# A streaming-encoder block on one Trainium2 core: the layer-norm boundaries between its stages are issued in another order, and the last whole feed-forward group stays in PSUM

## The chip, the core and the metric

The program runs on one core of a Trainium2 chip. TensorE (PE) multiplies 128 x 128 blocks into PSUM, VectorE (DVE) and ScalarE (ACT) do elementwise work, GpSimd (POOL) elementwise work in SBUF, and SyncE (SP) and ACT issue DMA transfers. Each engine works through its own queue in order. The metric is the device time of the whole program in microseconds (us), the median of several runs; smaller is better.

## The reference

One layer over 256 tokens of width 2048, in float32, with three sublayers, each closed by a layer norm:

```
x <- LN1(alpha*x + 1/2 * g1 * SwiGLU_1(mod1(x)))      feed-forward, D_FF = 5632
x <- LN2(alpha*x +       g2 * W_out[ mLSTM(u) || RG-LRU(u) ])   u = mod2(x)
x <- LN3(alpha*x + 1/2 * g3 * SwiGLU_2(mod3(x)))      feed-forward, D_FF = 5632
mod_s(x) = LayerNorm_noaffine(x) * (1 + scale_s(c)) + shift_s(c)
shift, scale, gate = silu(c) @ w_ada + b_ada
```

So between two sublayers the result y of the last product is scaled by the gate and added to x, x is normalized with gain and bias, normalized again without them, transposed, and scaled and shifted into `u`, which is the input of the next sublayer's first product.

## The kernel before, in words

The 256 tokens are two blocks (t = 0, 1) of 128 partitions. Every float32 weight tile (128 x 2048, 1 MB) is loaded by SP into one of four `raw` buffers (`load`, L80) and split into two float32r tiles: `hi` is a cast on ACT (L94), `lo` the rest, a subtraction on DVE (L96). A product is three matmuls (hi x hi, lo x hi, hi x lo). Activations are kept split and transposed in `uh` and `ul`. There are three pairs of `hi`/`lo` buffers; `spare` (two of six `slot` tiles) and the halves of `uh`/`ul` serve as more where a tile must be held. When a tile is in `fine` mode it is split in four pieces of 512 columns.

`w_ada`, from which shift, scale and gate come, is 144 further tiles of 1 MB (`ada_tile`, L163: one reducing DVE step each). `tick` puts them between the weight loads at a rate per stage (`RAMP_RATE`, `FFN1_RATE`, `MIX_RATE`, `FFN2_RATE`).

A feed-forward stage (`ffn`) takes its 44 column tiles in groups of eight; the last group has four. `g1` makes the hidden tiles of a group (`pg`, `pv`), `g2` multiplies them by the second weight into PSUM banks `py`, which DVE adds to `yacc` in SBUF (L599). When the last whole group has been added, `residual` multiplies `yacc` by the gate and adds it to x (L287, L288, both on POOL there). The last four tiles' share, the products `tl`, goes to `boundary`.

`boundary` runs three times: FFN1 to mixer, mixer to FFN2, and at the end of the kernel, where nothing follows. `products(t)` are the last products of block t. `take(t, n)` takes a 512-wide quarter of them: times the gate, added to x, and its statistics. `norm(t)` normalizes x with gain `ln_g` and bias `ln_b`: three quarters on DVE, the fourth on ACT and POOL, and `bn_stats` again for the second norm; `start_n`/`finish_n` make the normalized block `n`; `u_of(t, n, k)` transposes a quarter (512 columns, four transposes, `tu`) and scales it into `uh`/`ul`; `mov_t` multiplies the group by a tile of the next stage's weights (12 matmuls, PSUM bank `o` in the mixer, `fg` in FFN2). For block 0 these are done group by group, with the takes of block 1 between them; then comes the norm of block 1 and its groups. One or two of the four weight tiles that are not split ahead (`late`) are split between the groups.

The order of most instructions on an engine is found by a scheduler; those issued through `V`, `A`, `G` and `T` (`Pinned`, L108) keep the order in which they are written.

## Time and profile before

| | |
|---|---|
| median of 3 runs | 2080.53 us (2080.49 to 2081.13) |
| the profiled execution | 2079.97 us, its span 2078.2 us |
| PE busy | 1949.3 us, 94% of the span |
| DVE, ACT, POOL busy | 1434.1, 837.4, 132.7 us |
| PE's mean granted clock | 0.97 |
| moved by DMA | 513.27 MB, 247 GB/s |

The profile is of one execution. Busy times are sums of single instructions' spans; a wait is an engine's idle time, put down to what released it. Where all steps go through a helper, they have its line: L118 is every pinned instruction, so a row is told by the names of what it writes and reads (`x<-x,rsp,ln_b` is the bias step of the norm). Windows are stretches of the span. The granted clock is the share of its full rate that PE was given. The span in 40 slices of 52 us shows PE nearly full but for slices 0 and 1, 15 and 16, 24 and 25, and the last: the start, the two boundaries with a stage behind them, and the end.

### The profile page before, as it was taken

Reading aid. Unit: us, or ns where it says so; the run is one execution under the profiler, and the core shown is the slowest. Engines: PE = TensorE matmul, PEld = TensorE weight load, DVE = VectorE, ACT = ScalarE, POOL = GpSimd, SP = SyncE. Lnnn points to the kernel's source line nnn. Section 1 sums busy time; section 2 is a strip of 40 time slices with the busy share of each in tenths; the row PEclk is TensorE's granted clock in tenths of the full one; section 3 lists DMA queues with packets and bytes.
Section 4 is the critical chain, followed back from the end, with each engine's and each line's share of the span. In section 5 each row is a group of like instructions: output and inputs, shape, how many; then the busy total and the mean of one; then the engine's idle time right before and its main releaser. Section 6 shows DMA issues by size and latency. Waiting matters only on the chain. (4 is left out here: it accounts for less than half of the span.)

```text
span 2078.2 us, 30197 instructions
## 1 busy us (share of the span) xinstructions
PE 1949.3 (94%) x13068; PEld 1800.0 (87%) x13068; DVE 1434.1 (69%) x1287; ACT 837.4 (40%) x788; POOL 132.7 (6%) x111
## 2 busy tenths in 40 slices
PE   7999999999999995599999996799999999999996
PEld 6899998899998974399999884699999899899984
DVE  7998898988878797468876875355444544544558
ACT  5433344443333333443843343433343333333341
POOL 0000000000000071200000112000000000000024
PEclk9999999999999997799999998899999999999998
DMA  9998889998998983266687572366555555555552
GB/s 369 353 352 299 311 310 355 363 355 338 358 348 337 352 299 126 94 248 239 223 301 271 192 270 81 120 228 238 203 185 184 194 188 183 185 183 180 184 196 87
DMA packets 72709, 513.27 MB, mean 247 GB/s; under 512 B 8448, under 2 KB 8576, under 8 KB 10880
## 3 DMA queue, kind: packets, MB, share of 16 engines
q1 hardware_dynamic: 69984, 501.25, 65.5%
q10 hardware_dynamic: 2592, 10.09, 1.3%
q8 instruction: 102, 1.67, 0.3%
q14 instruction: 31, 0.25, 0.0%
HBM read 509.22 MB, written 2.10 MB: 246 GB/s over the span
## 5 line engine op out<-in xcount | busy, mean ns | idle before, releaser
L163 DVE CUSTOM_DVE_ANT_0 ada<-ada,scb,badac 128x2048 f32<-128x2048 f32 x144 | 341.8, 2376 | 20.4 <-DMA ada<-in_w_ada 18.3
L258 PE MATMUL pg<-uh,lg 128*128 128x256 f32 x960 | 272.0, 283 | 0.6 <-DVE lg L96 0.5
L96 DVE TENSOR_TENSOR lw<-rw,hw 128x2048 fp32r<-128x2048 f32 x80 | 185.7, 2321 | 125.4 <-ACT hw L94 125.3
L258 PE MATMUL pv<-uh,lv 128*128 128x256 f32 x960 | 271.8, 283 | 0.0
L256 PE MATMUL pg<-uh,hg 128*128 128x256 f32 x960 | 271.7, 283 | 0.0
L257 PE MATMUL pv<-ul,hv 128*128 128x256 f32 x960 | 271.7, 283 | 0.0
L256 PE MATMUL pv<-uh,hv 128*128 128x256 f32 x960 | 271.7, 283 | 0.0
L257 PE MATMUL pg<-ul,hg 128*128 128x256 f32 x960 | 271.7, 283 | 0.0
L268 PE MATMUL py<-lw,hth 128*128 128x512 f32 x640 | 250.2, 391 | 4.7 <-DVE lw L96 4.5
L269 PE MATMUL py<-hw,htl 128*128 128x512 f32 x640 | 249.2, 389 | 0.0
L267 PE MATMUL py<-hw,hth 128*128 128x512 f32 x640 | 242.7, 390 | 0.0
L96 DVE TENSOR_TENSOR lv<-rv,hv 128x2048 fp32r<-128x2048 f32 x68 | 155.8, 2291 | 123.4 <-ACT hv L94 123.3
L94 ACT CAST hw<-rw 128x2048 fp32r<-128x2048 f32 x80 | 152.7, 1911 | 215.5 <-DMA rw<-in_w 71.0
L96 DVE TENSOR_TENSOR lg<-rg,hg 128x2048 fp32r<-128x2048 f32 x60 | 137.5, 2292 | 106.4 <-ACT hg L94 106.4
L94 ACT CAST hv<-rv 128x2048 fp32r<-128x2048 f32 x68 | 129.4, 1905 | 194.7 <-PE pg L257 76.1
L258 PEld LDWEIGHTS pg<-uh,lg 128*128 128x128 f32 x960 | 184.2, 192 | 1.2 <-DVE lg L96 1.2
L256 PEld LDWEIGHTS pg<-uh,hg 128*128 128x128 f32 x960 | 184.2, 192 | 0.3
L257 PEld LDWEIGHTS pg<-ul,hg 128*128 128x128 f32 x960 | 184.2, 192 | 0.3
L258 PEld LDWEIGHTS pv<-uh,lv 128*128 128x128 f32 x960 | 184.3, 192 | 0.0
L256 PEld LDWEIGHTS pv<-uh,hv 128*128 128x128 f32 x960 | 184.3, 192 | 0.0
L257 PEld LDWEIGHTS pv<-ul,hv 128*128 128x128 f32 x960 | 184.3, 192 | 0.0
L94 ACT CAST hg<-rg 128x2048 fp32r<-128x2048 f32 x60 | 114.2, 1904 | 172.2 <-PE pv L257 108.3
(387 smaller groups left out, 4313.7 us busy)
## 6 DMA issues: line engine op xcount, KB each, us to landing
ada<-in_w_ada SPq DMA_DIRECT2D x144, 1024.0 KB, 5.8
rw<-in_w SPq DMA_DIRECT2D x80, 1024.0 KB, 4.8
rg<-in_w SPq DMA_DIRECT2D x60, 1024.0 KB, 5.0
rv<-in_w SPq DMA_DIRECT2D x60, 1024.0 KB, 4.8
rra<-in_w_r SPq DMA_DIRECT2D x48, 1024.0 KB, 5.5
rs<-in_w_s SPq DMA_DIRECT2D x32, 1024.0 KB, 4.9
rwo<-in_w_out SPq DMA_DIRECT2D x16, 1024.0 KB, 4.8
ro<-in_w_vo SPq DMA_DIRECT2D x8, 1024.0 KB, 4.9
```

Source lines behind the costliest of these rows:

```text
L94: act.copy(cut(hi, w), like(raw[:, w], hi))
L96: low.tensor_sub(cut(lo, w), like(raw[:, w], lo), cut(hi, w).bitcast(F32))
L163: nc.vector.tensor_tensor_reduce(raw, raw, scb, 1.0, badac[:, s, j, kt:kt + 1], ALU.mult, ALU.add, adac[:, s, j, kt:kt + 1])
L256: nc.tensor.matmul(ps, hi[:, w], uh[:, k0 + j, :], start=st, stop=False)
L257: nc.tensor.matmul(ps, hi[:, w], ul[:, k0 + j, :], start=False, stop=False)
L258: nc.tensor.matmul(ps, lo[:, w], uh[:, k0 + j, :], start=False, stop=sp)
L267: nc.tensor.matmul(o, acth[:, k0 + j, tk], cut(hi, w), start=first and j == 0, stop=False)
L268: nc.tensor.matmul(o, acth[:, k0 + j, tk], cut(lo, w), start=False, stop=False)
L269: nc.tensor.matmul(o, actl[:, k0 + j, tk], cut(hi, w), start=False, stop=last and j == 3)
```

## The change

1. *Last whole group in PSUM.* `g2_kept` replaces `g2` for group 4: its products go into eight banks `tl`, one for each block and quarter, which stay open, and the last four tiles' products are added there. The group's `yacc` adds are gone; `yacc` times gate goes into x one group earlier, now on DVE, without `w_ada` tiles beside it.
2. *The norm.* All four quarters are DVE steps. The bias step also writes the sum of its result (`accum_out`), and ACT sums the squares of (x + `sb`), `sb` being minus the mean of the bias; from both come mean and variance of the second norm. `bn_stats` for it are gone.
3. *The order.* `norm` and `takes` are generators, and `front` sets how many of block 1's steps stand between block 0's groups: its takes and its norm. Two quarters are transposed before group 0's products, and the products of a group stand behind the `u` steps of the next. The late weight tiles come in quarters, `hi` on ACT and `lo` on POOL.
4. *Loads.* `ln_g` and `ln_b` are loaded through SP, behind the weight tiles that are split ahead.
5. *Elsewhere.* The scaling of x is pinned on ACT and moved behind the first projections of the mixer; the `og` steps of the mixer come behind the boundary's last pinned instructions (`behind`). `w_ada` rates: FFN1 0.9 to 0.85, mixer 0.45 to 0.55; the shifts and scales of the next sublayer are completed before the boundary.

How the instructions move, first on PE behind the first boundary's last `tl` product. `tu` are the transposes of a quarter, `o` the products of the mixer's first tile, `ho`/`lo` its split weights. Before:

```order
L267 MATMUL tl_7221<-uh,hth_6258 128x512
L268 MATMUL tl_7221<-ul,hth_6258 128x512
L269 MATMUL tl_7221<-uh,htl_6259 128x512
L118 MATMUL tu_0_7275<-ident,n_7257 128x128 x4
L267 MATMUL o_7274<-ho_7136,uh 128x512
L268 MATMUL o_7274<-lo_7137,uh 128x512
```

And with the change:

```order
L279 MATMUL tl_6727<-uh,htl_6274 128x512
L120 MATMUL tu_0_7217<-ident,n_7213 128x128 x4
L120 MATMUL tu_1_7222<-ident,n_7213 128x128 x4
L120 MATMUL tu_2_7239<-ident,n_7213 128x128 x4
L277 MATMUL o_7214<-ho_7074,uh 128x512
L278 MATMUL o_7214<-lo_7075,uh 128x512
```

Three quarters are transposed ahead of the first product; the fourth follows two matmuls into the second group. Next DVE at the same boundary, from the end of block 0's first norm to the first quarter of `n` (`gy` and `sts` of 120 belong to block 1's takes). Before:

```order
L118 SCALAR_TENSOR_TENSOR x<-x,rsp_7238,ln_b_7074 128x512
L118 BN_STATS stp_7243<-x 128x6 x2
L118 BN_AGGR mvn_7258<-stp_7243 128x2
L118 TENSOR_TENSOR gy_7267<-tl_7182,gate 128x512
L118 TENSOR_TENSOR x<-x,gy_7267 128x512
L118 TENSOR_SCALAR n_7257<-x,mvn_7258,rsn_7262 128x512
L118 TENSOR_SCALAR u_0_7280<-tu_0_7275,adac 128x128
```

And with the change, where the four bias steps in a row and a take of block 1 stand ahead of this:

```order
L120 TENSOR_REDUCE tot_7197<-sq_7176 128x2
L120 TENSOR_SCALAR tot_7197<-tot_7197 128x2
L120 TENSOR_TENSOR tot_7197<-tot_7197,sb_7025 128x1
L120 SCALAR_TENSOR_TENSOR tot_7197<-tot_7197 128x1
L120 TENSOR_TENSOR gy_7209<-tl_6725,gate 128x512
L120 TENSOR_TENSOR x<-x,gy_7209 128x512
L120 BN_STATS sts_120<-x 128x6
L120 TENSOR_SCALAR n_7213<-x,tot_7197,rsn_7204 128x512
```

The statistics behind the bias steps are gone, and with the take ahead of these rows two of block 1's stand before `n`, one on each side of the four small steps on `tot`. Last ACT, in block 0's groups at that boundary. Before:

```order
L118 ACTIVATE n_7257<-x,nbn_7264,rsn_7262 128x512 x3
L118 ACTIVATE u_0_7280<-tu_0_7275,adac 128x128 x3
L294 ACTIVATE x<-x 128x2048
L118 CAST uh<-u_0_7280 128x4x128
L118 ACTIVATE u_1_7309<-tu_1_7304,adac 128x128 x4
```

And with the change:

```order
L120 ACTIVATE u_0_7231<-tu_0_7217,adac 128x128 x3
L120 CAST uh<-u_0_7231 128x4x128
L120 ACTIVATE n_7213<-x,nbn_7206,rsn_7204 128x512
L120 CAST ho_7244<-ro_7023 128x512 x2
L120 ACTIVATE u_1_7254<-tu_1_7222,adac 128x128 x3
```

The quarters of `n` are made one at a time where three stood together, the scaling of x is gone from between the `u` steps, and half a late weight tile (`ho`) stands there.

The diff, cut to its core:

```diff
-FFN1_RATE = 0.9
-MIX_RATE = 0.45
+FFN1_RATE = 0.85
+MIX_RATE = 0.55
...
+    @contextmanager
+    def behind():
+        with ExitStack() as stack:
+            for e in (V, A, G):
+                stack.enter_context(tc.issue_after(e.last.ins))
+            yield
...
-            nc.scalar.dma_start(r, a[w][s:s + 1, :].to_broadcast([P, D]))
+            nc.sync.dma_start(r, a[w][s:s + 1, :].to_broadcast([P, D]))
...
-        (nc.vector if sts else nc.gpsimd).tensor_mul(g, y, gate[:, c])
-        nc.gpsimd.tensor_add(x[:, t, c], x[:, t, c], g)
+        nc.vector.tensor_mul(g, y, gate[:, c])
+        (nc.gpsimd if sts else nc.vector).tensor_add(x[:, t, c], x[:, t, c], g)
...
         def norm(t):
-            mv, r, nb = moments_of(sts[t], f"p{s}{t}")
-            st = sm.tile([P, 4, 6], F32, tag="st", name=f"stp{s}{t}")
-            A.activation(x[:, t, cs[3]], x[:, t, cs[3]], AF.Identity, bias=nb, scale=r)
-            G.tensor_mul(x[:, t, cs[3]], x[:, t, cs[3]], g[:, cs[3]])
-            G.tensor_add(x[:, t, cs[3]], x[:, t, cs[3]], b[:, cs[3]])
-            for c in cs[:3]:
+            mv = sm.tile([P, 2], F32, tag="mv", name=f"mvp{s}{t}")
+            V.bn_aggr(mv, sts[t].rearrange("p a b -> p (a b)"))
+            r = rstd_in_order(mv[:, 1:2], f"p{s}{t}")
+            sq = sm.tile([P, 2, 4], F32, tag="sq", bufs=2, name=f"sq{s}{t}")
+            for c in cs:
                 V.scalar_tensor_tensor(x[:, t, c], x[:, t, c], mv[:, 0:1], g[:, c], op0=ALU.subtract, op1=ALU.mult)
+                yield
             for n, c in enumerate(cs):
...
+                    V.scalar_tensor_tensor(x[:, t, c], x[:, t, c], r, b[:, c], op0=ALU.mult, op1=ALU.add,
+                                           accum_out=sq[:, 0, n:n + 1])
+                    junk = sm.tile([P, 512], F32, tag="u", bufs=2, name=f"junk{s}{t}{n}")
+                    A.activation(junk, x[:, t, c], AF.Square, bias=sb, accum_out=sq[:, 1, n:n + 1])
...
+                yield
+            if following:
+                tot = sm.tile([P, 4], F32, tag="tot", bufs=2, name=f"tot{s}{t}")
+                V.tensor_reduce(tot[:, 0:2], sq, op=ALU.add, axis=mybir.AxisListType.X)
+                V.tensor_scalar_mul(tot[:, 0:2], tot[:, 0:2], 1.0 / D)
+                V.tensor_add(tot[:, 2:3], tot[:, 0:1], sb)
+                V.scalar_tensor_tensor(tot[:, 3:4], tot[:, 2:3], tot[:, 2:3], tot[:, 1:2], op0=ALU.mult,
+                                       op1=ALU.subtract)
+                r = rstd_in_order(tot[:, 3:4], f"n{s}{t}", -1.0)
+                mrb[t] = tot[:, 0:1], r, scaled_by(tot[:, 0:1], r, f"n{s}{t}")
+                yield
...
+        def late_split(k, part):
...
+            A.copy(hi[:, c], raw[:, c])
+            G.tensor_sub(lo[:, c], raw[:, c], hi[:, c].bitcast(F32))
...
+        def front(t, between):
+            n = slot(f"n{s}{t}")[:, 0:D]
+            pss.append(bank(f"{nm}{t}"))
+            n_of(t, n, 0)
+            n_of(t, n, 1)
+            pt = [turned(t, n, 0), turned(t, n, 1)]
+            for k in range(4):
+                between(k)
+                u_of(t, pt[k], k)
+                if k < 2:
+                    n_of(t, n, k + 2)
+                if k:
+                    mov_t(pss[t], fw[k - 1], uh, ul, (k - 1) * 4, t, k == 1, False)
+                if k < 2:
+                    pt.append(turned(t, n, k + 2))
+            mov_t(pss[t], fw[3], uh, ul, 12, t, False, True)
...
+            while ahead and (len(order[0]) == 1 or i == len(order[0]) // 2 or len(ahead) > 2):
+                low_ahead(ahead.pop(0))
             take(0, n)
...
+        A.activation(b, b, AF.Identity, accum_out=sb)
+        A.mul(sb, sb, -1.0 / D)
+        many = len(order[1]) > 1
+        other = chain(takes(1, order[1]), norm(1))
+        one = norm(0)
+        pieces = late_pieces()
+        run(one, 8)
+        if many:
+            run(other, 1)
+        run(one)
+        if many:
+            run(other, 1)
+        def beside(k):
+            run(pieces, (0, 2, 2, 0)[k] if len(late) == 1 else 2)
+            run(other, (1, 1, 3, 3)[k] if many else (1, 3, 3, 3)[k])
+        front(0, beside)
+        run(other)
+        front(1, lambda k: None)
...
+        def g2_kept(gi):
+            hth, htl = hts[gi]
+            for t in range(NT):
+                for n in range(4):
+                    ps_last[t, n] = bank(f"tl{s}{t}{n}")
+            for n in range(4):
+                for k in range(2):
+                    hl = load_w(w2[(2 * gi + k) * 4 + n], f"w2{s}_{2 * gi + k}_{n}")
+                    for t in range(NT):
+                        mov_t(ps_last[t, n], hl, hth, htl, k * 4, t, k == 0, False)
...
-            if gi:
+            if gi == len(groups) - 1:
+                g2_kept(gi - 1)
+            elif gi:
                 g2(gi - 1)
+                if gi == len(groups) - 2:
+                    credit[:] = 0.0, 0.0
+                    for t in range(NT):
+                        for n in range(4):
+                            residual(s, t, n, yacc[t][:, n * 512:(n + 1) * 512], None)
+        if following:
+            ada_until(s + 1, 1, KT - 1)
...
-        scale_x()
         nc.gpsimd.memset(xr[:, :, 0:3], 0.0)
         proj(1, 8, xr, {0: gates, 6: gate_cols})
+        scale_x()
```

More of the change, by code (lines that the diff above doesn't have):

```diff
@@ L1 @@
-from contextlib import ExitStack
+from contextlib import ExitStack, contextmanager
+from itertools import chain
 import numpy as np
@@ L318, in boundary @@
+    def boundary(s, ps, hls, order, mm, sts, following):
+        cs = [slice(c, c + 512) for c in range(0, D, 512)]
+        ready = ()
         if following:
             tiles, nm, ready, in_slots = following
-            fw = [load(tiles[k], f"{nm}{k}", spare if k in in_slots else None) for k in range(4)]
-            pss = []
-        else:
-            ready = ()
+            fw = [load(tiles[k], f"{nm}{k}", spare if k in in_slots else None) for k in range(4) if k in ready]
+        g, b = ln_rows(s)
+        if following:
+            fw += [load(tiles[k], f"{nm}{k}", None) for k in range(len(fw), 4)]
+            late = [k for k in range(4) if k not in ready]
+            sb = sm.tile([P, 1], F32, tag="sb", bufs=1, name=f"sb{s}")
@@ new lines, in run, with late_pieces @@
+        def run(steps, m=100):
+            for _ in range(m):
+                if next(steps, steps) is steps:
+                    return
+        def late_pieces():
+            for k in late:
+                for part in range(4):
+                    late_split(k, part)
+                    if part == 3:
+                        fw[k] = lates[k]
+                    yield
+        def front(t, between):
[14 more added lines that the diff above has]
+            mov_t(pss[t], fw[3], uh, ul, 12, t, False, True)
@@ L391, in boundary @@
+        mrb, lates, pss = {}, {}, []
         products(0)
+        ahead = list(ready)
         for i, n in enumerate(order[0]):
-            for k in ready[i:] if n == order[0][-1] else ready[i:i + 1]:
-                fw[k] = split(fw[k], nc.scalar, nc.vector)
+            while ahead and (len(order[0]) == 1 or i == len(order[0]) // 2 or len(ahead) > 2):
+                low_ahead(ahead.pop(0))
             take(0, n)
-            stats(sts[0], 0, n)
         products(1)
-        rest = list(order[1])
@@ L424, in boundary @@
-        n = finish_n(1, start_n(1, norm(1)))
-        pss.append(bank(f"{nm}1"))
-        for k in range(4):
-            u_of(1, n, k)
-            mov_t(pss[1], fw[k], uh, ul, k * 4, 1, k == 0, k == 3)
+            run(norm(0))
+            run(takes(1, order[1]))
+            run(norm(1))
+            return
+        A.activation(b, b, AF.Identity, accum_out=sb)
[3 more added lines that the diff above has]
+        one = norm(0)
```

131 lines of the change are left out of this document (54 added, 77 removed).

## Prediction

> **What bounds the kernel now.** The page comes first.
>
> ```profile
> span 2078.2 us, 30197 instructions
> PE 1949.3 (94%) x13068; PEld 1800.0 (87%) x13068; DVE 1434.1 (69%) x1287; ACT 837.4 (40%) x788; POOL 132.7 (6%) x111
> ```
>
> PE is busy 94% of the span, so only 129 us of it can be idle time, and the views that follow ask where that lies. The profiled execution took 2079.97 us: 1.77 us lie around its span, and it is 0.56 us under the median of the three runs (2080.53). PE's waits, longest first:
>
> ```profile
> PE tu L118 <- DVE n L118: 34.0, 4, 18.6
> PE o L267 <- ACT uh L118: 23.8, 7, 5.9
> PE fg L267 <- ACT uh L118: 21.5, 7, 4.7
> PE py L268 <- DVE lw L96: 4.5, 5, 1.0
> ```
>
> The first three rows, 79.3 us, are the two boundaries with something to prepare behind them (FFN1 to mixer, `o`; mixer to FFN2, `fg`). The table of windows gives their stages (columns: length, then busy us and instructions of PE, PEld, DVE, ACT, POOL; then granted clock, DMA share, GB/s):
>
> ```profile
> 728.00:778.90 50.90, 46.24 (x202) 36.47 (x201) 49.39 (x36) 17.04 (x17) 38.00 (x14) 1.00 0.84 301
> 778.90:801.00 22.10, 22.02 (x96) 17.94 (x96) 17.13 (x23) 8.12 (x17) 4.36 (x3) 1.00 0.56 209
> 801.00:886.50 85.50, 36.48 (x118) 26.29 (x117) 45.01 (x63) 35.08 (x63) 17.17 (x20) 0.68 0.27 92
> 819.60:851.80 32.20, 19.35 (x64) 13.84 (x64) 15.84 (x25) 14.96 (x30) 9.57 (x8) 0.76 0.17 52
> 856.20:886.50 30.30, 17.10 (x53) 12.45 (x53) 8.19 (x9) 14.88 (x22) 0.27 (x1) 0.68 0.24 84
> 1259.40:1327.50 68.10, 37.73 (x118) 27.31 (x118) 21.59 (x31) 30.25 (x58) 11.12 (x12) 0.72 0.22 77
> 1260.90:1292.60 31.70, 20.27 (x64) 14.53 (x64) 10.19 (x17) 16.55 (x34) 6.70 (x6) 0.78 0.19 66
> 2060.40:2078.20 17.80, 0.00 (x0) 0.00 (x0) 13.39 (x19) 1.31 (x3) 5.64 (x5) 0.59 0.24 88
> ```
>
> 801.0 is the end of the last `tl` product, 886.5 the moment from which PE runs without a gap. In those 85.5 us it does 118 instructions: seven weight groups of 12 matmuls and the transposes. At the pace of row 778.90 (96 matmuls in 22.1 us, 0.23 each) a group takes 2.75 and the whole about 22; 63 us are lost. At the second boundary (1259.4 to 1327.5) the same work costs 68.1, so 46 are lost. Part of that is the clock: the mean grant is 0.68 and 0.72.
>
> ```profile
> 824.84 0.80 PE L267 MATMUL o<-ho,uh 128*128 128x512 f32 x1 [4.05 <-ACT uh L118]
> 825.43 0.63 PE L268 MATMUL o<-lo,uh 128*128 128x512 f32 x1
> 825.86 0.63 PE L269 MATMUL o<-ho,ul 128*128 128x512 f32 x1
> 828.00 0.41 PE L268 MATMUL o<-lo,uh 128*128 128x512 f32 x1
> 838.00 0.60 PE L267 MATMUL o<-sh,uh 128*128 128x512 f32 x1 [2.25 <-ACT uh L118]
> 838.40 0.63 PE L268 MATMUL o<-sl,uh 128*128 128x512 f32 x1
> ```
>
> After 4.05 us of idling, matmuls start 0.43 us apart until 828.00, 3.2 us on; even after 2.25 the second comes 0.40 behind the first. Seven matmuls run in that spell, so a cold start costs 7 x 0.2 = 1.4 us, a group run wholly cold 12 x 0.2 = 2.4.
>
> **The change, part by part.** Prices of the steps at the first boundary:
>
> ```profile
> 793.48 2.50 DVE L96 TENSOR_TENSOR lo<-ro,ho 128x512 fp32r<-128x512 f32 x4 [4.75 <-ACT ho L94]
> 809.70 2.08 DVE L118 SCALAR_TENSOR_TENSOR x<-x,mvp,ln_g 128x512 f32<-128x512 f32 x3
> 811.70 0.75 DVE L118 SCALAR_TENSOR_TENSOR x<-x,rsp,ln_b 128x512 f32<-128x512 f32 x1
> 813.09 1.52 DVE L118 SCALAR_TENSOR_TENSOR x<-x,rsp,ln_b 128x512 f32<-128x512 f32 x1
> 817.63 0.26 DVE L118 BATCH_NORM_AGGREGATE mvn<-stp 128x2 f32<-128x24 f32 x1
> 819.08 0.54 DVE L118 TENSOR_SCALAR n<-x,mvn,rsn 128x512 f32<-128x512 f32 x1
> 819.22 2.22 ACT L118 ACTIVATE n<-x,nbn,rsn 128x512 f32<-128x512 f32 x3
> 821.35 1.13 ACT L118 ACTIVATE u<-tu,adac 128x128 f32<-128x128 f32 x3
> 822.38 1.91 ACT L294 ACTIVATE x<-x 128x2048 f32<-128x2048 f32 x1
> 824.18 0.61 ACT L118 CAST uh<-u 128x512 fp32r<-128x512 f32 x1
> 837.86 2.18 ACT L118 CAST ho<-ro 128x512 fp32r<-128x512 f32 x4
> 838.55 5.45 POOL L118 TENSOR_TENSOR lo<-ro,ho 128x512 fp32r<-128x512 f32 x4 [19.69 <-ACT ho L118]
> ```
>
> One 512-wide normalizing step is 0.69 (2.08/3) for the gain, 0.75 for the bias with POOL quiet and 1.52 with POOL working; from the aggregate to `n` 1.45 through POOL; on ACT `n` 0.74 a quarter, three `u` 1.13, `uh` 0.61, a quarter of a late weight tile 0.55, on POOL 1.36. The end of the kernel gives a price for `take` (two products and a statistic) and the norm:
>
> ```profile
> 2038.12 0.50 PE L267 MATMUL tl<-sh,hth 128*128 128x512 f32 x1 [2.48 <-ACT sh L94]
> 2046.48 0.69 DVE L118 TENSOR_TENSOR gy<-tl,gate 128x512 f32<-128x512 f32 x1 [3.15 <-PE tl L269]
> 2055.10 2.08 DVE L118 SCALAR_TENSOR_TENSOR x<-x,mvp,ln_g 128x512 f32<-128x512 f32 x3
> 2060.12 0.68 DVE L118 TENSOR_TENSOR gy<-tl,gate 128x512 f32<-128x512 f32 x1
> 2073.66 1.59 POOL L118 TENSOR_TENSOR x<-x,ln_b 128x512 f32<-128x512 f32 x1
> ```
>
> Four takes and an aggregate: 2055.10 - 2046.48 = 8.62, so 2.1 a take; the norm 2055.10 to 2060.12.
>
> *Last whole group in PSUM (FFN1, FFN2).* Sixteen DVE adds into `yacc` go (they don't hold PE), and the residual's 16 POOL steps become 16 DVE steps of 0.69, 11 us, one group earlier. They lie beside matmuls; DVE there now also loses the `w_ada` tiles, and if that cover failed they would cost up to 11 us. What goes is the end's crowding: in row 728.00 DVE is busy 49.4 of 50.9 us and PE idles 50.9 - 46.2 = 4.7. I take all of it as gained, since a weight tile's split (2.3 to 2.5 us on DVE) is then all that stands beside its 5.5 us of matmuls: **-4.7**. The wait `tl <- ACT sh` at 2038.12 (2.48) goes for the same reason, counted below.
>
> *First boundary.* Time 0 is the first `tl` product of the first token block. Before: products end at 22.1, PE is full at 107.6. Now: the first two takes follow their tiles (3.1, 5.9) and end at 8; two weight splits of 2.5 (row 793.48; their loads now stand ahead of the norm's two rows, which moved from ACT's queue into SP's behind them, so no load ends this wait; the rows themselves, and ACT's sum over one of them, 1.9 by row 822.38, have until 17 to be there) to 13; two takes to 17.1; aggregate 0.3; four gain steps 2.8; four bias steps with an accumulator 4 x (0.75 + 0.08) = 3.3, to 23.5. The squares run on ACT beside them. Then DVE's row holds a take of the second block (2.1), four tiny steps (estimate 1.0, from the aggregate's 0.26), and another take (2.1), which covers POOL's 1.45; `n` at 29.2. PE idles 7.1 instead of the 18.6 of its longest wait.
>
> *First block's u groups.* Now two transposes stand ahead of group 0's matmuls. Cold transposes 1.1; a take and the fourth `u` part on DVE 2.5; `uh` 0.6; `n` of the third quarter and its transposes 1.3: matmuls begin at 34.7 and run cold, 4.2. From there ACT sets the pace: per group `n` 0.74 + two late quarters 1.1 + `u` 1.13 + `uh` 0.61 = 3.6 against PE's 2.75. The fourth group has two squares instead of the late quarters and ends at 49. So 19.8 against 32.2 (row 819.60).
>
> *Second block's norm.* After the last `ul` (46.7) two bias steps, a square, the tiny steps and POOL's 1.45 are left: `n` at 52, PE idles 3 (before: 4.4). *Second block's u groups.* Nothing stands beside them: transposes and first `u` 4.1, one cold group 4.2, two warm ones 5.5, the last transposes 0.4: 14.2 against 30.3 (row 856.20); the two scalings of x (1.91 each, ACT) leave that path. PE is full at 66.2. For the four POOL splits I add half of 4 x (1.52 - 0.75): 1.5. 107.6 - 67.7 = **-40**.
>
> *Second boundary.* `n` comes no earlier: aggregate 0.3, gain 2.8, bias 3.3, square 0.75, tiny 1.0, POOL 1.45 and `n` make 10.1, as now. Eight late quarters and the whole second norm stand beside the first block's groups: the 19.8 from above, 2.2 for four more late quarters, 1.5 for the last steps of that norm and a second cold start, 1.4, make 25 against 31.7 (row 1260.90). The second block's `n` is then there as soon as PE is: 13.4, as above less some of the cold transposes. Contention of eight splits 3. From 1259.4: 1.5 + 25 + 13.4 + 3 = 43 against 68.1: **-25**.
>
> *End of the kernel.* PE reaches `tl` 2.5 earlier, at 2035.6. The fourth tile is taken at 13.5 (PE sets that), norm 0.3 + 2.8 + 3.0 = 6.1, four takes 8.3, norm 6.1, and the 2.95 between the last step (2073.66 + 1.59) and the end: 37, so 2072.5 instead of 2078.2: **-5.7**.
>
> *Rates.* The order of SP has 17 fewer `w_ada` tiles in FFN1, 7 more in the mixer, 10 more in FFN2.
>
> ```profile
> 886.50:1237.00 350.50, 350.19 (x2321) 322.14 (x2320) 270.39 (x317) 164.11 (x175) 16.50 (x23) 1.00 0.69 250
> L163 DVE CUSTOM_DVE_ANT_0 ada<-ada,scb,badac 128x2048 f32<-128x2048 f32 x144 | 341.8, 2376 | 20.4 <-DMA ada<-in_w_ada 18.3 <-ACT scb L145 1.8
> L163 DVE DVE_READ_ACCUMULATOR2_ANT adac<- 128x1 f32 x144 | 12.0, 83 | 0.0
> ```
>
> Each is 2.46 us of DVE. The mixer has 350.5 - 270.4 = 80 us of DVE to spare, and seven take 17: 0, and at most 17 if they land on the one chain. The ten in FFN2, 25 us of DVE over some 700, are costed at nothing too: they lie beside matmuls, and 25 is what they cost if that fails.
>
> Sum: 4.7 + 40 + 25 + 5.7 = 75.4 off 2079.97 is 2004.6, as a median 2005.
>
> Five cold starts are in the sum, after the gaps over 3 us. Row 838.00 would charge one more to each of four fourth groups, whose `uh` comes some 2 us late: 4 x 1.4 = 5.6, 2010. I leave them out, since PE is busier between these gaps than before, and keep 5.6 for the upper end. The Trainium skill, "TensorE: Matmul & The Clock Gate", section "Why this matters for your kernels", says that only gaps over some 3 us bring the slow clock back; by that rule the sum stays 2005, and row 838.00 disagrees with it. The Trainium skill's "Vector Engine (DVE) Microarchitecture Reference", section 7, says that a scalar-tensor-tensor with two fp32 sources and an accumulator runs at half rate; no run here shows that form, and the reducing row L163 (2376 ns for 2048, 0.6 per 512) is not halved.
>
> What has no row: the accumulating bias step, between 0.83 (taken, by L163) and 1.52 (the contended row), which is rival 2; a square with an accumulator, 0.74 (`n`) to 1.0 (with a further small ACT step), 1 us in all; the tiny steps, 0.1 to 0.3 each, 3 us in all; POOL's contention, none to whole, 4.5 either way; no cold start but the first of each boundary, 3 x 1.4 less and two groups' rest, 6 in all.
>
> **Rivals.**
> 1. *The clock stays low.* Groups of 2.75 every 3.6 us leave PE a quarter idle, and row 838.00 shows a short gap ending cold. Of the eleven groups counted warm, five in the first blocks' fronts would cost 5.1 - 3.6 = 1.5 more and six in the second blocks' 2.4: +22, 2027. Against: a cold group takes 5.1, so gaps close and the clock returns, as within each group now. 0.14.
> 2. *The accumulating step takes 1.52.* Fourteen of the sixteen stand on the path (four and two at the first boundary, four and four at the second): 14 x 0.7 = 10, 2015. For: two fp32 inputs already slow down when POOL shares the time; against: L163. That is what the Vector Engine page of the Trainium skill would make of it. 0.12.
> 3. *Slower: DVE becomes the mixer's bound.* PE has no idle time there (350.2 of 350.5), so each us by which DVE's work exceeds 350 delays the end one for one. It binds once 80 us are added, and makes the kernel slower only past 155; seven tiles (17) and the `og` steps that now wait behind the boundary (4 x 1.4) bring 23. Against it, then, by a factor of seven; what speaks for it is only chains inside that window that the mean hides. With 165 added, 2090. 0.03.
> 4. *No gain:* the pinned rows make ACT's chain as long as the old gaps. It would take 10 us more a front than 3.6 a group allows. 2080. 0.01.
>
> **How the numbers follow.** Forecast 0.70, rivals 0.14, 0.12, 0.03, 0.01. Its own range is 2005 less 6 + 4.5 + 3 (1991) and plus 5.6 + 4.5 + 3 + 1 (2019); rival 2 lies in it, and rival 1 reaches 2027 and a little more. 1990 to 2031 leaves out less than 2 in 10. A measurement of this kernel tells some 0.2% (4 us) from no change: faster 0.96, same 0.01, slower 0.03.
>
> **What would show it.** Right: PE's wait for the first `n` near 7 us at the first boundary and unchanged at the second; from the last `tl` product to gapless PE 46 and 43; no `py` or `tl` wait at either FFN's end; the last out transfer some 37 us after the first `tl` product. Accumulating steps of 0.75 and clean PE windows in the mixer settle rivals 2 and 3; a granted clock under 0.75 through both fronts is rival 1. Wrong: if fronts take over 25 us with a full clock, if PE idles in the mixer, or if `tl` waits for banks.

## The result, and the profile after

The changed kernel takes 2036.5 us (median of 4 runs, 2034.03 to 2037.31), beside 2080.83 for the kernel before in the same session: a ratio of 0.9781, 95% interval 0.9764 to 0.9798. It is faster by 44 us, where 75 were forecast, and it lies 5.5 us above the forecast's range. The profiled execution took 2036.97 us, its span 2035.2.

The page of the profile after (in the last row each digit is PE's busy share, in tenths, in a slice of 51 us):

```profile
span 2035.2 us, 30179 instructions
PE 1952.9 (96%) x13068; PEld 1797.4 (88%) x13068; DVE 1425.5 (70%) x1335; ACT 838.0 (41%) x794; POOL 51.3 (3%) x71
PE   7899999999999998897999997999999999999997
```

PE has the same 13068 instructions and 47 us less idle time, but there is a dent that before did not have, in slice 18 (counted from 0; 916 to 967 us), inside the mixer. PE's waits name it (the rows of the mixer and the boundaries):

```profile
PE pcol L819 <- DVE gg L810: 13.8, 1, 13.8
PE tu L120 <- ACT n L120: 10.7, 4, 3.2
PE fg L277 <- ACT uh L120: 8.6, 3, 4.2
PE tu L120 <- DVE n L120: 7.9, 3, 5.4
...
PE o L277 <- ACT uh L120: 2.6, 2, 1.7
```

The waits `tl <- ACT sh` are gone, the longest wait for an `n` is 5.4 us instead of 18.6, and the longest wait of the program is a new one: the transposes into `pcol` (the mLSTM's gate columns) wait 13.8 us for DVE's chain of small gate steps on `gg`.

To see where the 43 us of span come from, cut both spans into the same six stretches: to the end of FFN1's `tl` products; from there to `pif`, the first product behind the first boundary's; to the last `pw` product; to the last `fv` product; to the first weight tile of the last `tl`; to the end. The changed kernel's windows:

```profile
0.00:800.80 800.80, 777.24 (x5375) 724.10 (x5376) 654.33 (x582) 330.13 (x286) 4.01 (x13) 0.99 0.84 317
800.80:871.00 70.20, 55.09 (x226) 43.48 (x225) 47.55 (x66) 39.41 (x69) 9.76 (x14) 0.88 0.41 148
871.00:1213.30 342.30, 328.46 (x2212) 303.81 (x2212) 270.16 (x320) 154.89 (x165) 15.57 (x23) 0.98 0.70 260
1213.30:1309.10 95.80, 80.01 (x322) 62.71 (x322) 56.80 (x79) 49.15 (x86) 18.62 (x18) 0.89 0.38 143
1309.10:1999.00 689.90, 689.56 (x4842) 645.48 (x4841) 369.14 (x249) 264.43 (x190) 0.00 (x0) 1.00 0.58 209
1999.00:2035.20 36.20, 22.54 (x97) 17.84 (x95) 27.53 (x42) 0.00 (x0) 3.38 (x4) 0.88 0.16 58
```

The same cuts in the kernel before lie at 800.6, 911.1, 1237.3, 1351.7 and 2038.1. Its window of FFN2:

```profile
1351.70:2038.10 686.40, 683.59 (x4842) 645.36 (x4840) 345.70 (x218) 259.48 (x186) 23.06 (x14) 1.00 0.55 195
```

All six side by side:

| stage | before | after | difference | forecast |
|---|---|---|---|---|
| FFN1 with its `tl` | 800.6 | 800.8 | +0.2 | -4.7 |
| first boundary | 110.5 | 70.2 | -40.3 | -40 |
| mixer | 326.2 | 342.3 | +16.1 | 0 |
| second boundary | 114.4 | 95.8 | -18.6 | -25 |
| FFN2 | 686.4 | 689.9 | +3.5 | -2.5 |
| end, from the first `tl` | 40.1 | 36.2 | -3.9 | -3.2 |
| span | 2078.2 | 2035.2 | -43.0 | -75.4 |

(The last two forecasts are the two parts of the -5.7 for the end.) Four of the six rows miss, and two stages that were to stay or gain got longer: the mixer, and FFN2, in which PE is busy for 689.6 of 689.9 us, 6 us more than before for the same products. A stage in which PE hardly waits and which still takes longer has slower products; that is a different fault from the mixer's.

### The profile page after: what moved, and what is told of

The parts are those of the page before. It is cut to its first block, busy times and chain, and to the rows that moved or that the text cites. A ratio compares the mean times of both kernels' runs of the same rounds, so it can differ in the third digit from the quotient of the medians.

```text
span 2035.2 us, 30179 instructions
## 1 busy us (share of the span) xinstructions
PE 1952.9 (96%) x13068; PEld 1797.4 (88%) x13068; DVE 1425.5 (70%) x1335; ACT 838.0 (41%) x794; POOL 51.3 (3%) x71
## 4 chain that ended last, share of the span: by engine, by line
PE 86%; DVE 8%; issue 2%; ACT 2%; DMA 2%; POOL 0%; DVEq 0%; SPq 0%; POOLq 0%; ACTq 0%
PE pv L266 6%; PE pv L267 6%; PE pg L268 6%; PE pg L266 6%; PE pv L268 6%; PE pg L267 6%; PE py L278 6%; PE py L279 6%; PE py L277 6%; PE pj L266 2%; PE pj L268 2%; PE pj L267 2%; DVE x L120 2%; PE tl L278 2%; PE tl L279 2%
## 5 line engine op out<-in xcount | busy, mean ns | idle before, releaser
L173 DVE CUSTOM_DVE_ANT_0 ada<-ada,scb,badac 128x2048 f32<-128x2048 f32 x144 | 337.8, 2348 | 31.7 <-DMA ada<-in_w_ada 29.9
L278 PE MATMUL py<-lw,hth 128*128 128x512 f32 x512 | 203.5, 398 | 2.1 <-DVE lw L97 2.1
L279 PE MATMUL py<-hw,htl 128*128 128x512 f32 x512 | 201.7, 394 | 0.0
L277 PE MATMUL py<-hw,hth 128*128 128x512 f32 x512 | 197.1, 395 | 0.0
```

What stands on the lines that cost most here:

```text
L173: nc.vector.tensor_tensor_reduce(raw, raw, scb, 1.0, badac[:, s, j, kt:kt + 1], ALU.mult, ALU.add, adac[:, s, j, kt:kt + 1])
L277: nc.tensor.matmul(o, acth[:, k0 + j, tk], cut(hi, w), start=first and j == 0, stop=False)
L278: nc.tensor.matmul(o, acth[:, k0 + j, tk], cut(lo, w), start=False, stop=False)
L279: nc.tensor.matmul(o, actl[:, k0 + j, tk], cut(hi, w), start=False, stop=last and j == 3)
```

## The experiments

Each run stands beside runs of the kernel before on the same chip (medians 2082.1 to 2083.4) and has four executions. The stage times are cut as above, from the profile of the run, which is one of the four.

**Where the slots lie.** The change adds three small tiles (`sq`, `tot`, `sb`) to a pool that lies ahead of the six large slots, which move by 160 bytes; `uh`, `ul`, x and the weight tiles stay. In the built programs the third slot starts at byte 193952 of a partition before and at 194112 after, `uh` at 43424 in both. So the remainder modulo 64 is 32 for all of them before; after, it is 0 for the slots and 32 for the others. Four kernels move tiles and nothing else: every engine's instructions stand in the same order. Three of them have a longer dummy column in this line:

```diff
-        gcol = sm.tile([P, 104], F32, tag="gcol", bufs=1, name="gcol")[:, 0:8]
+        gcol = sm.tile([P, 112], F32, tag="gcol", bufs=1, name="gcol")[:, 0:8]
```

*slots_plus_32*, the changed kernel with this line. 

> The changed kernel with its six large slots (hth, htl, n, rh, sh) 32 bytes further on, by a longer dummy column in the small pool; every engine's instructions and their order are the same. Theory (alignment): the change's new small tiles moved the slots from 32 to 0 modulo 64 bytes against uh, ul and the weight tiles, which stayed at 32, and a matmul whose stationary operand is a slot then takes 0.2335 us instead of 0.2270. 2112 of them in the two FFNs and some 190 in the mixer: 2300 x 0.0065 = 15 us less, about 2022, with tl and py products back at 0.227. Rival (the granted clock is a little lower since PE idles less): no change, 2036. Second rival (chance of this build): a change in another place than those products.

Measured: 2025.48 us, ratio 0.9725 (0.971 to 0.9739), 11 less than the changed kernel; FFN1 with `tl` 796.3, FFN2 685.8, the other stages within 2.2 us of the changed kernel's.

*slots_plus_64*, the same with 120. 

> The same with 64 bytes: the slots stay at 0 modulo 64. Theory (alignment modulo 64): no change, 2036, products of the slots still at 0.2335. Rival (it is the place of the slots as such, whatever the remainder): it moves by some us. By the clock rival: 2036 as well.

Measured: 2034.96, 0.9773 (0.9757 to 0.979): no change.

*before_slots_plus_32*, the line in the kernel before. 

> The kernel before with its slots 32 bytes further on, so from 32 to 0 modulo 64; the order of instructions is the same. Theory (alignment): 15 us slower, about 2095, with py and tl products at 0.2335 instead of 0.227. Rival (clock): no change, 2080.

Measured: 2092.07 beside 2082.3, 1.0044 (1.0027 to 1.0061): slower by 10; its FFN1 4.4 and its FFN2 5.6 longer.

*others_plus_32*: a column at the very start is made longer, so that everything moves.

```diff
-    mhalf = cst.tile([P, 1], F32, name="mhalf")
+    mhalf = cst.tile([P, 16], F32, name="mhalf")[:, 0:1]
```

> The changed kernel with all tiles 32 bytes further on (a longer column at the start): uh, ul and the weight tiles go from 32 to 0 modulo 64 and the slots from 0 to 32; the order is the same. If it matters that the two operands of a product lie at the same remainder, the products of slots stay slow: 2035. If it matters that the stationary operand (or the slots) lies at 32, they are at 0.227 again, but uh's products would be the slow ones: FFN products with w13, 256 wide, may show it; 2025 or less is then possible.

Measured: 2036.9, 0.9777 (0.9762 to 0.9791): as slow as the changed kernel, although the slots' remainder modulo 64 is 32 again, since the others' is now 0.

One row for each kernel shows it, the products `py<-hw,htl` of the groups by line and shape (total us, mean ns of one). A 128x128 block of `htl`, in a slot, is the stationary operand; the weight tile `hw` streams past it. Before:

```profile
L269 PE MATMUL py<-hw,htl 128*128 128x512 f32 x640 | 249.2, 389 | 0.0
```

The kernel before with its slots moved by 32:

```profile
L269 PE MATMUL py<-hw,htl 128*128 128x512 f32 x640 | 253.1, 395 | 0.0
```

The changed kernel, and then with its slots moved by 32:

```profile
L279 PE MATMUL py<-hw,htl 128*128 128x512 f32 x512 | 201.7, 394 | 0.0
```

```profile
L279 PE MATMUL py<-hw,htl 128*128 128x512 f32 x512 | 200.3, 391 | 0.0
```

In *others_plus_32* products of `ul` with weight tiles have both operands at remainder 0, and keep the old rate:

```profile
L279 PE MATMUL po<-ho,ul 128*128 128x512 f32 x32 | 12.5, 389 | 0.0
```

The clock rival falls: with the same instructions in the same order, on one chip, 32 bytes make the difference between 2034.96 (*slots_plus_64*) and 2025.48 (*slots_plus_32*). What counts is how the two operands of a product lie to each other, not where either lies. But 391 is not 389, so the remainder modulo 64 is not all; the last two runs below take that up.

**The wait in the mixer.** *ada_later* keeps the number of `w_ada` tiles in the mixer and starts them later.

```diff
-MIX_RATE = 0.55
+MIX_RATE = 0.68
...
-                credit[:] = -2.0, MIX_RATE
+                credit[:] = -9.0, MIX_RATE
```

> The changed kernel, with the mixer's w_ada tiles starting later: none among the eight weight tiles behind pif (five now), as many in the whole mixer (credit starts at -9 with a rate of 0.68). Theory: PE's wait of 13.8 us at pcol comes from the w_ada steps (2.43 us each, and up to 2.5 us of waiting for their loads) that stand in DVE's row between the steps of the gate chain; with five of them gone the chain ends 12 to 18 us earlier, the wait goes and with it a cold start: about 2021. Rival (the chain is late because PE now comes sooner and DVE's row is full of weight splits and conv steps): the wait shrinks by less than a third, 2032 or more.

Measured: 2022.53, 0.9711 (0.9694 to 0.9728), 14 less; the mixer takes 328.1 instead of 342.3 and the wait at `pcol` is gone. What stood in the way is seen in DVE's row of the changed kernel, from the first step of the gate chain (`gg`) on:

```profile
883.92 0.41 DVE L713 SCALAR_TENSOR_TENSOR gg<-gg 4x256 f32<-4x256 f32 x1
884.61 2.29 DVE L97 TENSOR_TENSOR ls<-rs,hs 128x2048 fp32r<-128x2048 f32 x1 [0.29 <-ACT hs L95]
886.82 0.27 DVE L715 TENSOR_SCALAR gg<-gg 4x256 f32<-4x256 f32 x1
889.15 2.35 DVE L173 CUSTOM_DVE_ANT_0 ada<-ada,scb,badac 128x2048 f32<-128x2048 f32 x1 [2.06 <-DMA ada<-in_w_ada]
891.43 0.08 DVE L173 DVE_READ_ACCUMULATOR2_ANT adac<- 128x1 f32 x1
891.43 1.74 DVE L716 RECIPROCAL gg<-gg 4x256 f32<-4x256 f32 x1
...
899.04 2.35 DVE L173 CUSTOM_DVE_ANT_0 ada<-ada,scb,badac 128x2048 f32<-128x2048 f32 x1 [1.63 <-DMA ada<-in_w_ada]
...
932.43 0.41 DVE L808 SCALAR_TENSOR_TENSOR gg<-gg 4x256 f32<-4x256 f32 x1
```

And in *ada_later*:

```profile
883.42 0.41 DVE L713 SCALAR_TENSOR_TENSOR gg<-gg 4x256 f32<-4x256 f32 x1
...
890.38 1.75 DVE L721 SCALAR_TENSOR_TENSOR gg<-gg 4x256 f32<-4x256 f32 x4
...
901.82 0.41 DVE L808 SCALAR_TENSOR_TENSOR gg<-gg 4x256 f32<-4x256 f32 x1
```

From L713 to L808 the chain needs 48.5 us in the one and 18.4 in the other. Its steps are short and each needs the one before; in a row that is fixed, every 2.35 us tile between two of them, and every wait of that tile for its load (2.06, 1.63), is added to the chain. Four tiles (2.43 each with their accumulator's read) and these two waits make 13.4 of the 30.1 us between the two chains; the rest is that eight weight splits (`ls`) stand between the steps instead of three, and more conv steps (`xc`), since the row was ordered anew around the tiles. In the kernel before, three tiles stood in this chain, none waited for its load, and it took 35.6 us (921.12 to 956.72). The same stretch by engine, first of the changed kernel and then of *ada_later*:

```profile
884.00:936.00 52.00, 39.03 (x326) 38.82 (x324) 47.85 (x68) 18.68 (x18) 0.00 (x0) 0.92 0.75 279
```

```profile
884.00:936.00 52.00, 52.00 (x435) 51.85 (x435) 47.13 (x66) 24.15 (x21) 0.00 (x0) 1.00 0.68 239
```

DVE is as busy in both (47.9 and 47.1 of 52 us). Its busy share doesn't tell the kernels apart; the order of its work does.

*rates_back* undoes the change's own rates.

```diff
-FFN1_RATE = 0.85
-MIX_RATE = 0.55
+FFN1_RATE = 0.9
+MIX_RATE = 0.45
```

> The changed kernel with the old rates (FFN1 0.9, mixer 0.45); 27 w_ada tiles fall into the mixer instead of 30, three behind pif ahead of rs8 instead of five. Theory (the w_ada steps in DVE's row lengthen the gate chain, and the change's own rate put them there): two steps of 2.43 us and their waits for loads, some 2 us each, leave the chain: PE's wait at pcol falls from 13.8 to about 5, 2027. Rival (the chain is late because PE comes sooner, whatever the rate): the wait stays over 10, 2034.

Measured: 2021.1, 0.9702 (0.9687 to 0.9716); mixer 327.0, no wait at `pcol`. The theory expected too little (a wait of 5 was to be left, and none is); its cause is confirmed: the boundary's new order does not need these rates, and they cost 15 us. How much of it is the steps' own time and how much their late loads was not told apart.

*mended* has both repairs, the longer column (112) and the later tiles. 

> The changed kernel with both: slots 32 bytes further on, and w_ada tiles later in the mixer. If the two costs are separate they add: 11 (measured) and 14 (measured) off 2036.5, 2011.5; left over against the forecast of 2005 is the second boundary. Rival (a mixer that runs faster meets its DVE chain again): the wait at pcol comes back in part, 2016 or more.

Measured: 2013.56, 0.9667 (0.9651 to 0.9683). They add: 23 of the 31 us by which the forecast was short.

**The parts of the boundary**, each undone or altered in *mended* (boundaries there 70.8 and 95.1 us). The loads of `ln_g` and `ln_b` and the moved scaling of x were not undone by themselves, so what they bring is not shown.

*u_first*: a group's `u` steps are issued ahead of the second block's norm steps.

```diff
             for k in range(4):
                 between(k)
                 u_of(t, pt[k], k)
+                after(k)
...
-        def beside(k):
+        def early(k):
             run(pieces, (0, 2, 2, 0)[k] if len(late) == 1 else 2)
+
+        def beside(k):
             run(other, (1, 1, 3, 3)[k] if many else (1, 3, 3, 3)[k])
 
-        front(0, beside)
+        front(0, early, beside)
```

> The mended kernel with each group's u steps ahead of the steps of the second block's norm, on every engine, instead of behind them. Theory: at the second boundary PE waits 4.2 and 4.1 us (and starts cold after each) because in ACT's row the third and fourth group's u steps stand behind squares that wait for DVE, whose bias steps take 1.75 us beside POOL's splits, and behind the reciprocal root's way through POOL; freed of that, PE gains 6 to 8 us there and 2 at the first boundary: 2003. Rival (the second block's n comes later by what the first block's groups gain, since DVE and ACT do the same work): 0 to -2, 2010.

Measured: 2003.97, 0.9621 (0.9607 to 0.9636), 9.6 less: second boundary 88.5, first 71.4 (nothing gained there). The profiled execution, the slowest of its four, is 6.1 shorter than that of *mended*, and the second boundary's 6.6 account for that.

*none_ahead*: no transposes ahead.

```diff
-            pt = [turned(t, n, 0), turned(t, n, 1)]
             for k in range(4):
+                pt = turned(t, n, k)
                 between(k)
-                u_of(t, pt[k], k)
+                u_of(t, pt, k)
                 if k < 2:
                     n_of(t, n, k + 2)
-                if k:
-                    mov_t(pss[t], fw[k - 1], uh, ul, (k - 1) * 4, t, k == 1, False)
...
+                mov_t(pss[t], fw[k], uh, ul, k * 4, t, k == 0, k == 3)
```

> The mended kernel (2013.6) without the transposes ahead: each group's four transposes stand right behind the matmuls of the group before, as in the kernel before. Theory (the lead is the main gain at the boundaries): then PE idles in each group for the u steps (1.15 + 0.4), the uh cast (0.6) and a transpose (0.5), some 3 us, and the next group runs cold (2.4): three groups of each second front lose 4 to 5 us, of each first front, which ACT paces, 2: 2 x (13 + 6) = +38, 2050. Rival (ACT's work sets the pace of the groups anyway): +10 at most, 2023.

Measured: 2045.24, 0.9822 (0.9808 to 0.9837), 32 more: boundaries 91.7 and 106.3. Of the parts undone here the lead is the largest. PE's waits show the hole in each group:

```profile
PE fg L277 <- ACT uh L120: 21.8, 7, 4.8
PE o L277 <- ACT uh L120: 21.5, 7, 4.9
```

*norm_whole*: between the first block's groups stand only the takes, and the norm comes whole behind them.

```diff
-            run(other, (1, 1, 3, 3)[k] if many else (1, 3, 3, 3)[k])
+            run(other, (1, 1, 0, 0)[k] if many else (1, 0, 0, 0)[k])
```

> The mended kernel with the second block's norm whole behind the first block's last group instead of in steps between its groups. Theory: aggregate, gains, biases, last square, sums, POOL's root and n, some 11 us, then stand between the two blocks instead of the 2.3 to 5.7 us that PE waits there now; the first block's groups gain 2 to 3 us by it, since no norm step delays their u: +5 each, +10, 2024. Rival (the steps between the groups cost as much as they hide): 0, 2014.

Measured: 2004.3, 0.9627 (0.9612 to 0.9641), 9 **less**, where the theory had 10 more and its rival none: boundaries 69.7 and 87.3. The norm in steps, as the change places them, costs time. Why, is read at the second boundary. The changed kernel, the second norm's gain and first two bias steps on DVE, POOL's split beside them, ACT's squares and the `u` behind them, and PE:

```profile
1240.79 4.13 DVE L120 SCALAR_TENSOR_TENSOR x<-x,mvp,ln_g 128x512 f32<-128x512 f32 x3
1247.20 1.85 DVE L120 SCALAR_TENSOR_TENSOR x<-x,rsp,ln_b 128x512 f32<-128x512 f32 x1
1248.98 1.75 DVE L120 SCALAR_TENSOR_TENSOR x<-x,rsp,ln_b 128x512 f32<-128x512 f32 x1
1247.20 2.98 POOL L120 TENSOR_TENSOR lfg<-rfg,hfg 128x512 fp32r<-128x512 f32 x2 [1.59 <-ACT hfg L120]
1249.09 0.72 ACT L120 ACTIVATE junk<-x,sb 128x512 f32<-128x512 f32 x1 [1.44 <-DVE x L120]
1250.84 0.72 ACT L120 ACTIVATE junk<-x,sb 128x512 f32<-128x512 f32 x1 [0.93 <-DVE x L120]
1251.56 1.14 ACT L120 ACTIVATE u<-tu,adac 128x128 f32<-128x128 f32 x3
1253.84 0.80 PE L277 MATMUL fg<-hfg,uh 128*128 128x512 f32 x1 [4.19 <-ACT uh L120]
```

*norm_whole*, the gain steps, the first bias step, and PE's wait before the second block:

```profile
1231.22 2.74 DVE L120 SCALAR_TENSOR_TENSOR x<-x,mvp,ln_g 128x512 f32<-128x512 f32 x4
1233.88 0.75 DVE L120 SCALAR_TENSOR_TENSOR x<-x,rsp,ln_b 128x512 f32<-128x512 f32 x1
1240.02 1.97 PE L120 MATMUL tu<-ident,n 128*128 128x128 f32 x8 [5.18 <-DVE n L120]
```

Two things are paid for in the steps. First, beside POOL's splits two of the three gain steps take 1.77 instead of 0.69 (the third, in the same row, takes 0.75), and a bias step takes 1.75 to 1.85 instead of 0.75. The Trainium skill, "SBUF — State Buffer", section "SBUF: two separate sides", says that a DVE instruction with two SBUF inputs and a POOL instruction that reads SBUF lock each other out; the trace agrees, with these numbers. Second, ACT's row is fixed as well: `u` at 1251.56 stands behind two squares that wait 1.44 and 0.93 us for those slow bias steps, and PE, which waits for `uh`, starts 4.19 us late and cold. Taken whole, the norm finds POOL quiet, costs a wait of 5.18, and no product of the groups before it waits for `uh`.

*u_first* gained as much with the norm still in steps, so it is not the steps as such that cost, but steps that stand ahead of `u`. The two costs were not told apart: in *u_first* most of the contention went as well, since POOL's splits then lay for the most part beside other work:

```profile
1232.26 0.74 DVE L120 SCALAR_TENSOR_TENSOR x<-x,rsp,ln_b 128x512 f32<-128x512 f32 x1
```

*bn_stats*: the second statistic by `bn_stats` on DVE, as before (the column is lengthened so that the slots lie as in *mended*).

```diff
-                                           accum_out=sq[:, 0, n:n + 1])
-                    junk = sm.tile([P, 512], F32, tag="u", bufs=2, name=f"junk{s}{t}{n}")
-                    A.activation(junk, x[:, t, c], AF.Square, bias=sb, accum_out=sq[:, 1, n:n + 1])
+                    V.bn_stats(st[:, n, :], x[:, t, c])
```

> The mended kernel with the second statistic taken by four statistics instructions of 0.69 us on DVE and one aggregate, as before, instead of accumulating bias steps, squares on ACT and four small sums. Theory (the squares are a small part of the gain): the first norm gets 4 x 0.6 longer on DVE less the wait for the last square (1.0) and three small sums (0.6), so +1 at each first norm; the groups lose the squares from ACT's row and gain the statistics in DVE's: between -4 and +4 in all, 2010 to 2018. Rival (the squares off DVE carry the boundary): +10, 2024.

Measured: 2014.23, 0.9671 (0.9657 to 0.9686): no difference from *mended* that can be told (first boundary 2.6 longer, second 1.9 shorter).

*no_kept*: the last whole group goes through `yacc`, the residual through POOL, as before.

```diff
-            if gi == len(groups) - 1:
-                g2_kept(gi - 1)
-            elif gi:
+            if gi:
                 g2(gi - 1)
...
+                    if gi == len(groups) - 2:
+                        residual(s, t, n, yacc[t][:, c], None)
```

> The mended kernel with the last whole ff group of each FFN added into yacc and the residual on POOL behind it, as before. Theory (the forecast's first and last terms): PE's idling of some 4 us at FFN1's end and 2.5 us at FFN2's end comes back: +7, 2020.5. Rival (that idling was covered or is made up behind it): 0.

Measured: 2026.88, 0.9735 (0.9718 to 0.9751), 13 more, twice the 7 expected: FFN1 with `tl` 3.2 longer, first boundary 5.6, FFN2 2.5, end 3.3. The crowding delays not only the products but the takes behind them: the wait for the first `n` is 9.8 instead of 5.7.

**Best version.** *norm_whole* with the slots moved further: 128 in the `gcol` line (96 bytes on from the changed kernel's place) and 192 (352 bytes).

> The mended kernel with the second norm whole (2004.3) and its slots 96 bytes on from the change's place instead of 32, so that slots, uh and weight tiles have the same remainder modulo 256; the order is the same. With 32 the slots' products lay between: 0.391 to 0.394 a record, 0.389 before, 0.394 to 0.398 in the changed kernel, and FFN1 ended 4 us earlier than in the changed kernel where 4.7 + 6 were due. Theory (the remainder counts beyond 64): products of slots at 0.389, 2300 x 0.0017 = 4 us less, 2000. Rival (64 is all that counts): 2004.

> The same with 352 bytes: equal modulo 512 as in the kernel before. If only an equal remainder modulo 512 restores the old rate: 2000, and the run with 96 bytes stays at 2004; if 128 or 256 suffice, both are at 2000.

Measured: 2000.13, 0.961 (0.9594 to 0.9626), and 2000.38, 0.9611 (0.9596 to 0.9625), 4 below *norm_whole*. The products in *whole_equal_256*:

```profile
L279 PE MATMUL py<-hw,htl 128*128 128x512 f32 x512 | 199.3, 389 | 0.0
```

They are at 389 again. An equal remainder modulo 256 is enough; 512 adds nothing. Whether 128 would do was not tried. Why the place counts at all is not shown: the runs show the cost, not the mechanism. These are the fastest kernels here, 82 us under the kernel before and 36 under the changed one.

## Why the prediction was wrong, step by step

**The ends of the FFNs (-4.7 and -2.5): right in themselves, hidden by a cost that the sum put at nothing.** PE's idle time fell by 4.8 us in FFN1 and by 2.5 in FFN2 (span less busy time in the windows), as said. But 2112 products of the two FFNs became some 6 ns slower each, because three small tiles had moved the slots: FFN1 took 0.2 us more instead of 4.7 less, FFN2 3.5 more instead of 2.5 less. With the slots set right (*whole_equal_256*) FFN1 with its `tl` takes 793.8, so -6.8, and FFN2 683.7, so -2.7. The place costs 15 us in all: 11 (*slots_plus_32*) and 4 (*whole_equal_256*). The sum counted instructions and waits and took it that a product costs the same in both kernels.

**First boundary (-40): -40.3, a hit by luck in part, since errors cancel.** To the first transposes 5.8 us instead of 19.0 (-13.2; forecast -11.5: the wait for `n` was 5.4, not 7.1); the first block's groups 23.4 instead of 32.2 (-8.8; forecast -10.9, by ACT's pace and the 1.5 for POOL's splits); then 2.3 instead of 4.4 (forecast 3); the rest -16.2 (forecast -16.1). The third group began after a gap of 1.68 and ran mostly cold, 4.9 us instead of 2.75; cold starts after such short gaps are what the prediction left out ("I leave them out"). These rows show it (PE; starts and waits):

```profile
806.62 1.97 PE L120 MATMUL tu<-ident,n 128*128 128x128 f32 x8 [5.40 <-DVE n L120]
820.96 0.50 PE L277 MATMUL o<-sh,uh 128*128 128x512 f32 x1 [1.68 <-ACT uh L120]
832.31 1.09 PE L120 MATMUL tu<-ident,n 128*128 128x128 f32 x8 [2.29 <-DVE n L120]
```

**Second boundary (-25): -18.6.** The step that failed is "the 19.8 from above, 2.2 for four more late quarters, 1.5 for the last steps of that norm and a second cold start, 1.4, make 25": the first block's groups took 32.3 (1236.15 to 1268.40), as long as before (31.7). All else there came as forecast (what follows was 59.1 before and is 40.7, -18.4, forecast -18.5). The step added up ACT's work and did not ask what ACT's fixed row makes it wait for, and it priced the contention of eight splits at 3 where six slow steps of the norm alone cost 6 us of DVE. *u_first* and *norm_whole* show the size of the error: 6.6 and 7.8 less at this boundary.

**Rates (0, at most 17): +16.1.** The step that failed is "0, and at most 17 if they land on the one chain". They did: the gate chain had to be at `pcol` in 52 us, before made it without a wait, and now came 13.8 late. That the cost lies so near the bound is chance: the 17 was the DVE time of seven tiles, and the chain was held up by four, two waits for their loads and the splits that fell in between. The prediction had "if PE idles in the mixer" among its signs of being wrong. The 80 us of DVE to spare in the mixer were real and no help.

**End (-3.2 of the -5.7): -3.9**, since takes and norm came as priced.

**The rivals.** The clock stayed low in one half of the fronts. These are the first and second block's groups, at the first boundary and then at the second (the granted clock is the third figure from the end):

```profile
806.60:830.00 23.40, 18.57 (x64) 13.66 (x64) 17.18 (x29) 13.36 (x30) 7.26 (x6) 0.75 0.27 93
832.30:848.00 15.70, 13.06 (x59) 10.76 (x60) 8.04 (x9) 13.40 (x22) 0.21 (x1) 0.89 0.15 50
1236.10:1268.40 32.30, 20.44 (x64) 14.79 (x65) 19.29 (x29) 17.29 (x38) 13.48 (x12) 0.74 0.35 130
1268.40:1285.00 16.60, 13.81 (x60) 11.08 (x59) 6.52 (x9) 11.78 (x21) 0.00 (x0) 0.88 0.15 50
```

Before, the first block's groups had 0.76 and 0.78, the second block's 0.68 and, at the second boundary (1299.9 to 1327.5), 0.64. So the first half of rival 1 came true, at its sign of 0.75, and its second half, the larger part of its price, did not. The accumulating step does not take 1.52: with POOL quiet it takes 0.75, and 0.08 for the accumulator's read, as taken; beside POOL's splits it takes 1.75 to 1.85, at the second boundary. The Trainium skill's "Vector Engine (DVE) Microarchitecture Reference", section 7, says that such a step with two non-bf16 sources in SBUF runs at half the rate; that is not seen here, nor in the gain step without an accumulator (0.69):

```profile
798.53 0.74 DVE L120 SCALAR_TENSOR_TENSOR x<-x,rsp,ln_b 128x512 f32<-128x512 f32 x1
799.20 0.08 DVE L120 DVE_READ_ACCUMULATOR x<-x,rsp,ln_b 128x1 f32 x1
```

The slower rival named its own exception, "chains inside that window that the mean hides", and that exception came true without DVE ever being the mixer's bound.

## What to carry to other kernels

A stage's spare time on an engine says nothing about a chain of short dependent steps in that engine's fixed row: ask, for each such chain, what stands between its steps, what that waits for, and when its last step is due. Where two stages of work are interleaved by hand, the other engines' rows are interleaved with them, and steps that look free can take more than twice their time beside POOL's (here 1.77 us instead of 0.69) or push the urgent step behind a wait; here the simpler order, with the norm in one piece, was 9 us better, and so was the one that kept the steps but put them behind the urgent `u`. And before times of two builds are compared step by step, see whether a product that nobody touched still costs the same in both.

## What the runs showed of the hardware

- The place of operands in SBUF changes the pace of products by 3%: the `py` products of FFN1 (128x512, float32r) start 0.227 us apart in the kernel before and 0.233 apart with the stationary operand's address moved by 32 bytes (*before_slots_plus_32*); their records go from 389 to 395 ns. The `py` records are at 389 to 391 where both operands have the same remainder modulo 256, and at 391 to 394 where only that modulo 64 is the same (*slots_plus_32*). The Trainium skill, "SBUF — State Buffer", section "SBUF: two separate sides", says that only the port pair of DVE and POOL causes contention among the engines and that PE never waits on anyone; what these runs show is a cost between the two operands of one product, with no other engine in it.
- A gap of 1.68 us in PE's work (the row at 820.96) was followed by matmuls 0.43 us apart from 822.28 to 824.84, one of 0.92 (at 826.74) by matmuls 0.23 apart from the fifth on. The gap of some 3 us that the Trainium skill's "TensorE: Matmul & The Clock Gate", section "Why this matters for your kernels", names for the slow clock's return is not borne out as a lower bound by the first of these; the forecast had priced cold starts for gaps over 3 us only.
